# Seven products for eight: a third of an FFN's down projection by Strassen's scheme

## The chip, the core and the metric

The kernel runs on one core of a Trainium2 chip. The metric is the device time of one execution in microseconds; the time given is the median of several executions. The core has five engines with a queue each: TensorE (PE), VectorE (DVE), ScalarE (ACT), GpSimd (POOL) and SyncE (SP). Each works through its own queue in order, and they meet at semaphores.

## What is computed

Two blocks in a row on x, 256 tokens by 1024 columns, float32. The first is a Conformer-like block, and its FFN occurs twice:

```
def swiglu_ffn(x, w_gate, w_up, w_down):
    return (jax.nn.silu(x @ w_gate) * (x @ w_up)) @ w_down

x = x + 0.5 * swiglu_ffn(rmsnorm(x, ffn1_norm), ffn1_w_gate, ffn1_w_up, ffn1_w_down)
x = x + hybrid_mixer(rmsnorm(x, mix_norm), w_in, ...)
x = x + 0.5 * swiglu_ffn(rmsnorm(x, ffn2_norm), ffn2_w_gate, ffn2_w_up, ffn2_w_down)
x = rmsnorm(x, final_norm)
```

The second block is two attention mixers with layer norms ("fox", then "dsa"). The change concerns `@ w_down` in both FFNs: h, 256 x 2816, times a matrix of 2816 x 1024.

## The kernel before

**Precision.** Each float32 operand is cut in two parts, a rounded one (`hi`, type fp32r) and the rest (`lo`). A product is three matmuls: hi by hi, lo by hi, hi by lo.

**Weights.** The weights of the whole kernel are a list of units in the order of use, `unit_list`. A down unit is two k-tiles (of 128 rows each) by 512 columns: 128 x 1024 in the core's memory, 512 KB. `load` (line 205) puts it into one of four `raw` buffers over SP's queue (`N_RAW`). `prefetch` (line 187) casts it on ACT (`whi`, line 198) and subtracts on DVE (`wlo`, line 199), into one of eight pairs of buffers (`N_W`), at most eight units ahead of use (`AHEAD`). A raw buffer is free again when its `wlo` is written, a `whi`/`wlo` pair when PE has used it. `half` (line 216) multiplies one token tile (128 of the 256 tokens, t = 0 or 1) by one unit: six matmuls of 128x512, by way of `mm` (line 164, profile line L165).

**An FFN** (`ffn`, line 378) goes through gate and up in five chunks of 512 hidden columns and one of 256. Each chunk of h is written by DVE in 32x32 blocks transposed (`hb`, line 420). `regroup` sends it from POOL's queue through memory: four transfers `d<-hb` (line 285) and, once they have landed, one `hd<-d` (line 286). Later `put_h` cuts hd into `hh` on ACT and `hl` on DVE (`split_psum`, lines 240 and 241). These are h transposed, the stationary operands of down. `pin` keeps an instruction in the order of the program; `later` queues work for a time at which enough matmuls have been issued by the planner's count (`DUE`). The other instructions are put in order by a scheduler.

**Down** comes next. There are two halves n of 512 columns; in each, 11 units by two token tiles, 132 matmuls; 264 in an FFN. After the last unit of a half, x is added to (line 440). After the first half, `x_T(t, 0)` is queued: PE transposes half of x, DVE scales it (`xg`, line 247), ACT casts it (`xh`, line 248), DVE subtracts (`xl`, line 249). That is input of the next stage, the mixer ("mix") or the second block's first layer.

Of the kernel before, what the change touches and what calls it, by code (L numbers as in the profile page):

```python
# [9 lines left out]
F32 = mybir.dt.float32  # L10
# [23 lines left out]
AHEAD = 8  # L34

# [8 lines left out]
          (0, 512), (512, 512), (1768, 512), (2280, 512)]  # L44


def unit_list():

    u = []

    def block(m, c0, w, k0=0, k1=KT, n=None):
        n = n or (UK * (512 // w) if 512 % w == 0 else UK)
        for k in range(k0, k1, n):
            u.append((m, k, min(n, k1 - k), c0, w))

    def ffn(i):
        for c0, w in FFN_CH:
            block(f"gate{i}", c0, w, n=1 if i == 1 and c0 == 0 else None)
            block(f"up{i}", c0, w)
        for n in range(2):  # L60
            block(f"down{i}", 512 * n, 512, 0, FT)
# [26 lines left out]
    "ffn_x": 3.0,  # L88
    "mix_T": 9.32,
# [26 lines left out]
class Kern:  # L116
    def __init__(self, ctx, tc, A):
# [11 lines left out]
        self.raw, self.W = {}, {}  # L129
# [57 lines left out]
    def prefetch(self, splits):  # L187
        nc = self.nc
        for _ in range(splits):
            if self.n_split < min(len(UNITS), self.used + AHEAD):  # L190
                self.load(self.n_split)
                i = self.n_split
                raw = self.raw.pop(i)
                nk, w = UNITS[i][2], UNITS[i][4]
                hi = self.wp.tile([P, UK * 512], F32R, name="whi", tag="whi", bufs=N_W)
                lo = self.wp.tile([P, UK * 512], F32R, name="wlo", tag="wlo", bufs=N_W)
                m = nk * w
                nc.scalar.copy(hi[:, :m], raw[:, :m])  # L198
                nc.vector.tensor_sub(lo[:, :m], raw[:, :m], hi[:, :m].bitcast(F32))  # L199
# [5 lines left out]
    def load(self, upto):  # L205
        while self.n_dma <= min(upto, len(UNITS) - 1):
            i = self.n_dma
            m = UNITS[i][2] * UNITS[i][4]
            raw = self.wp.tile([P, UK * 512], F32, name="raw", tag="raw", bufs=N_RAW)
            w = self.A["w"]  # L210
            self.nc.sync.dma_start(out=raw[:, :m], in_=bass.AP(
                tensor=w.tensor, offset=w.offset + self.off[i], ap=[[m, P], [1, m]]))
            self.raw[i] = raw
            self.n_dma += 1

# [16 lines left out]
    def done(self, n):  # L232
        self.used = n

# [143 lines left out]
    def ffn(self, u, gain, next_gain):  # L378
        nc, tc = self.nc, self.tc
        with tc.tile_pool(name="ffn", bufs=1, reuse_waits="tile") as pool:  # L380
# [3 lines left out]

            def put_h(j, n, hd):
                for t in range(2):
# [40 lines left out]
            nd = FT // UK  # L427
            for n in range(2):
                accs = [self.bank("mm") for _ in range(2)]
                for i in range(nd):  # L430
                    if n == 0 and i == nd - 2:
                        self.drain()
                    for t in range(2):
                        self.half(accs[t], hT[t], u + i, i == 0, i == nd - 1)
                    self.done(u + i + 1)
                    self.prefetch(1)
                u += nd
                for t in range(2):
                    xs = self.x[t][:, 512 * n:512 * n + 512]
                    nc.vector.tensor_add(xs, xs, accs[t])  # L440
                    if n == 0:
                        self.later(DUE["ffn_x"], lambda t=t: self.x_T(t, 0, next_gain))
# [752 lines left out]
def layout(inp):  # L1195
# [15 lines left out]
    for m, k0, nk, c0, w in UNITS:  # L1211
        b = mats[m][k0 * P:(k0 + nk) * P, c0:c0 + w]
# [33 lines left out]
```

## Time and profile before

| | |
|---|---|
| median of 3 runs | 720.14 us (718.51 to 721.09) |
| the profiled execution | 717.48 us |
| its span in the trace | 715.7 us |
| mean granted clock of PE | 0.996 |
| PE busy | 98% of the span |
| DVE busy | 69% |
| ACT busy | 52% |
| POOL busy | 9% |

The span reaches from the first to the last instruction in the trace; 1.78 us of the profiled execution lie outside it. Down runs from 129.40 to 190.15 us in the first FFN and from 397.72 to 458.49 us in the second. In a row of the trace an instruction's duration reaches from its start to its end; those of one engine overlap a little, so the step from one to the next is shorter than the duration. A bracket says how long the engine had stood idle before the row and what ended it.

### The profile page before, as it was taken

How to read it: one execution, taken by the hardware profiler on the slowest of the kernel's cores; microseconds unless marked ns; L12 is line 12 of the kernel's file. 1: busy time of each engine (PE TensorE's matmuls, PEld its weight loads, DVE VectorE, ACT ScalarE, POOL GpSimd, SP SyncE). 2: the span in 40 equal slices, each digit the busy share in tenths (PEclk: the TensorE clock that was granted, in tenths of full speed). 3: DMA queues.
4: the chain of work that ended last, by engine and by line, in shares of the span. 5: the costliest groups of instructions: out<-in, count | busy, mean ns of one | idle time of the engine just before them, and what ended most of it. 6: DMA issues, size and time to landing. Idle time of an engine off the chain costs nothing.

```text
span 715.7 us, 9843 instructions
## 1 busy us (share of the span) xinstructions
PE 701.6 (98%) x3594; PEld 590.0 (82%) x3594; DVE 491.4 (69%) x790; ACT 368.8 (52%) x552; POOL 62.2 (9%) x90
## 2 busy tenths in 40 slices
PE   8999999999999999999999999999999999999995
PEld 6788888888888778888888888888898888778984
DVE  5867765576547878655865576555456968997965
ACT  6664544364546646353544364555465635675820
POOL 0101110200002001011110200000300001000001
PEclk9999999999999999999999999999999999999998
DMA  8888566876744435558656867555672527543501
GB/s 257 311 313 301 209 217 212 302 229 221 254 151 145 178 115 172 194 197 290 208 209 220 293 229 228 175 192 174 206 253 77 159 83 230 195 123 114 177 1 59
DMA packets 42305, 140.87 MB, mean 197 GB/s; under 512 B 5512, under 2 KB 6672, under 8 KB 42128
## 3 DMA queue, kind: packets, MB, share of 16 engines
q1 hardware_dynamic: 37728, 127.23, 52.9%
q0 software_dynamic: 4096, 12.60, 5.0%
q8 instruction: 28, 0.46, 0.3%
q10 hardware_dynamic: 432, 0.41, 0.2%
q14 instruction: 21, 0.17, 0.1%
HBM read 133.39 MB, written 6.82 MB: 196 GB/s over the span
## 4 chain that ended last, share of the span: by engine, by line
PE 89%; DVE 4%; DMA 4%; ACT 2%; issue 1%; POOL 0%; SPq 0%; DVEq 0%; ACTq 0%; POOLq 0%
PE mm L165 80%; PE sc L165 5%; PE tr L180 3%; DMA raw<-in_w 1%; DVE wlo L199 1%; DMA rope<-in_rope 1%; PE tr L165 1%; DMA xin<-in_xT 1%; ACT whi L198 1%; DMA gain<-in_gain 0%; ACT s L452 0%; DVE sel L994 0%; DVE sel L1003 0%; ACT xh L323 0%; DVE s L543 0%
## 5 line engine op out<-in xcount | busy, mean ns | idle before, releaser
L199 DVE TENSOR_TENSOR wlo<-raw,whi 128x1024 fp32r<-128x1024 f32 (+3 forms) x236 | 274.3, 1177 | 83.0 <-ACT whi L198 73.4
L198 ACT CAST whi<-raw 128x1024 fp32r<-128x1024 f32 (+3 forms) x236 | 235.2, 1013 | 126.9 <-PE mm L165 65.7
L165 PE MATMUL mm<-whi,xh 128*128 128x512 f32 (+3 forms) x760 | 288.4, 380 | 1.9 <-ACT whi L198 1.9
L165 PE MATMUL mm<-wlo,xh 128*128 128x512 f32 (+3 forms) x760 | 283.4, 373 | 0.1
L165 PE MATMUL mm<-whi,xl 128*128 128x512 f32 (+3 forms) x760 | 283.4, 373 | 0.0
L165 PEld LDWEIGHTS mm<-whi,xh 128*128 128x128 f32 x760 | 143.2, 188 | 25.7 <-ACT whi L198 3.7
L165 PEld LDWEIGHTS mm<-wlo,xh 128*128 128x128 f32 x760 | 143.1, 188 | 25.5 <-DVE wlo L199 1.9
L165 PEld LDWEIGHTS mm<-whi,xl 128*128 128x128 f32 x760 | 143.3, 189 | 22.4 <-DVE xl L249 0.2
L165 PE MATMUL mm<-whi,hh 128*128 128x512 f32 x176 | 68.7, 390 | 0.0
L165 PE MATMUL mm<-whi,hl 128*128 128x512 f32 x176 | 68.5, 389 | 0.0
L165 PE MATMUL mm<-wlo,hh 128*128 128x512 f32 x176 | 68.5, 389 | 0.0
L241 DVE TENSOR_TENSOR hl<-hd,hh 128x512 fp32r<-128x512 f32 (+1 forms) x24 | 14.5, 644 | 59.4 <-ACT hh L240 59.4
L240 ACT CAST hh<-hd 128x512 fp32r<-128x512 f32 (+1 forms) x24 | 12.9, 583 | 67.0 <-DMA hd<-d 67.0
L285 POOL DMA_DIRECT2D d<-hb x48 | 26.5, 558 | 149.2 <-DVE hb L420 149.1
L165 PEld LDWEIGHTS mm<-wlo,hh 128*128 128x128 f32 x176 | 33.0, 188 | 6.9
L165 PEld LDWEIGHTS mm<-whi,hh 128*128 128x128 f32 x176 | 33.1, 188 | 6.8
L165 PEld LDWEIGHTS mm<-whi,hl 128*128 128x128 f32 x176 | 33.1, 188 | 6.7
L407 ACT ACTIVATE th<-mm,hr 128x512 f32<-128x512 f32 (+1 forms) x24 | 15.5, 648 | 19.9 <-PE mm L165 18.8
L452 ACT ACTIVATE s<-s,nmax 128x128 f32<-128x128 f32 (+1 forms) x48 | 21.3, 446 | 7.0 <-DVE nmax L450 7.0
L299 POOL TENSOR_TENSOR rs<-ms,mhalf 128x1 f32<-128x1 f32 x10 | 6.5, 652 | 169.7 <-DVE ms L312 169.7
L299 POOL TENSOR_TENSOR lr<-ve,mhalf 128x1 f32<-128x1 f32 x4 | 4.0, 991 | 167.6 <-DVE ve L651 167.6
L409 DVE SCALAR_TENSOR_TENSOR a<-th,mm 128x512 f32<-128x512 f32 (+1 forms) x24 | 15.1, 628 | 5.0 <-ACT th L407 5.0
(219 smaller groups left out, 598.6 us busy)
## 6 DMA issues: line engine op xcount, KB each, us to landing
raw<-in_w SPq DMA_DIRECT2D x208, 512.0 KB, 4.6
d<-hb POOLq DMA_DIRECT2D x40, 128.0 KB, 4.7
hd<-d POOLq DMA_DIRECT2D x10, 512.0 KB, 6.5
raw<-in_w SPq DMA_DIRECT2D x12, 344.0 KB, 3.4
raw<-in_w SPq DMA_DIRECT2D x8, 372.0 KB, 3.5
raw<-in_w SPq DMA_DIRECT2D x8, 256.0 KB, 4.4
x<-in_x SPq DMA_DIRECT2D x2, 512.0 KB, 6.6
B<-in_bias SPq DMA_DIRECT2D x1, 1024.0 KB, 5.5
```

Of the source, the lines that this page charges most:

```text
L165: self.nc.tensor.matmul(out, a, b, start=start, stop=stop)
L180: self.nc.tensor.transpose(out, a, self.ident[:p, :p])
L198: nc.scalar.copy(hi[:, :m], raw[:, :m])
L199: nc.vector.tensor_sub(lo[:, :m], raw[:, :m], hi[:, :m].bitcast(F32))
L240: i = nc.scalar.copy(hi, src)
L241: j = nc.vector.tensor_sub(lo, src, hi.bitcast(F32))
L285: self.nc.gpsimd.dma_start(out=d[a].rearrange("b i m -> i b m"), in_=src[32 * a:32 * a + 32])
L299: self.nc.gpsimd.tensor_tensor(out, a, self.mhalf[:, 0:1].to_broadcast(list(a.shape)), op=ALU.pow)
L407: nc.scalar.activation(th[:, :w], acc[:, :w], AF.Tanh, scale=hr[t])
L409: nc.vector.scalar_tensor_tensor(a[t][:, :w], th[:, :w], 1.0, acc[:, :w], op0=ALU.add, op1=ALU.mult)
L452: nc.scalar.activation(s[:, h, :], s[:, h, :], AF.Exp, bias=m[:, h:h + 1], accum_out=l[:, col + h:col + h + 1])
```

## The change

The first eight of the 22 k-tiles of h and of w_down are seen as two by two blocks: A11, A12, A21, A22 (128 tokens by 512 hidden columns) and B11 to B22 (512 rows by 512 columns). Seven products of sums of such blocks stand for the eight plain ones:

| product | of h | of the weights | goes to |
|---|---|---|---|
| P1 | A11 | B11 | x(0,0), m |
| P5 | A21 − A22 | B11 + B12 | x(0,1), x(1,1) |
| P6 | a sum of blocks | P5's + B22 | m, then x(0,1) |
| P7 | A11 − A21 | B12 + B22 | m, then x(1,0), x(1,1) |
| P2 | A12 | B21 | x(0,0) |
| P4 | A22 | P6's + B21 | x(1,0) |
| P3 | a sum of blocks | B22 | x(0,1) |

Signs are taken up in the sums; x(t, n) is token tile t, column half n. Each product is 12 matmuls, in two halves g of two k-tiles (`prod`), so 84 for 96. The 14 other k-tiles stay direct, as 14 units. The list `DOWN` sets the order: six direct units, then products and direct units by turns, then two direct units.

- Eight weight blocks of 512 KB are loaded in place of the eight units, not into raw buffers but to stay: b11 and b12 in the buffers of the old x transposed, b22 in those of hb, b21 in those of hd. b11, b12 and b22 are loaded when down opens.
- Their sums are made on DVE in place (line 230), eight of 128x1024 in each FFN. Each product half is split like a unit, 14 instead of 8.
- The four sums of h and their splits are made during gate and up, from the time at which the second chunk's h is cut, 2 us apart by the planner's count (`DUE["ffn_sum"]`); one split of h that nobody needs falls away.
- Additions to x (line 542): 13 of 128x512 instead of 4 in each FFN; one copy into m (ACT) and two additions to m (DVE).
- `x_T(t, 0)` is queued behind P4.

The core of the diff:

```
+AHEAD_P = 5
+DOWN = [(0, 8), (1, 8), (0, 10), (1, 10), (0, 12), (1, 12), "P1", (0, 14), "P5", (1, 14), "P6", (0, 16), "P7",
+        (0, 18), "P2", (0, 20), "P4", (1, 16), "P3", (1, 18), (1, 20)]
...
             if self.n_split < min(len(UNITS), self.used + AHEAD):
-                self.load(self.n_split)
                 i = self.n_split
-                raw = self.raw.pop(i)
+                if i in RECIPE and (not self.open_down or RECIPE[i][0] == "P1" and i >= self.used + AHEAD_P):
+                    break
+                self.load(i)
                 nk, w = UNITS[i][2], UNITS[i][4]
+                if i in RECIPE:
+                    what, g = RECIPE[i]
+                    w = 512
+                    _, add, key = PROD[what]
+                    raw = self.block[key, g]
+                    if add:
+                        self.pin(nc.vector.tensor_add(raw, raw, self.block[add[1], g]))
+                else:
+                    raw = self.raw.pop(i)
...
+                a = nc.scalar.copy(hi[:, :m], raw[:, :m])
+                b = nc.vector.tensor_sub(lo[:, :m], raw[:, :m], hi[:, :m].bitcast(F32))
+                if i in RECIPE:
+                    self.pin(a), self.pin(b)
...
+    def prod(self, acc, lhs, i):
+        if i not in self.W:
+            self.prefetch(i + 1 - self.n_split)
+        hi, lo = self.W[i]
+        g = RECIPE[i][1]
+        xh, xl = lhs
+        for k in range(2):
+            kk = 2 * g + k
+            self.mm(acc, xh[:, kk, :], hi[:, k, :], kk == 0, False, 1)
+            self.mm(acc, xl[:, kk, :], hi[:, k, :], False, False, 1)
+            self.mm(acc, xh[:, kk, :], lo[:, k, :], False, kk == 3, 1)
+        self.pump()
...
+            self.fpool, self.block, self.open_down = pool, {}, True
+            for i in range(u, len(UNITS)):
+                if i in RECIPE and RECIPE[i][0] in ("P1", "P5", "P6") and UNITS[i][0] == UNITS[u][0]:
+                    self.load_block(i)
...
+            for what in DOWN:
+                if what in PROD:
+                    acc = self.bank("sc")
+                    for g in range(2):
+                        self.prod(acc, lhs[what], u)
+                        u += 1
+                        self.done(u)
+                        self.prefetch(2)
+                    if what == "P1":
+                        nc.scalar.copy(m, acc)
+                    elif what in ("P6", "P7"):
+                        nc.vector.tensor_add(m, m, acc)
+                    for t, n, op in goes[what]:
+                        to_x(t, n, m if what in ("P6", "P7") else acc, op)
+                    if what == "P4":
+                        for t in range(2):
+                            self.later(DUE["ffn_x"], lambda t=t: self.x_T(t, 0, next_gain))
+                    continue
```

What stands in a row on three engines and places. First ACT's queue around the last h casts of the first FFN (`hh0` and `hh1` are the casts for the two token tiles, of the chunk of 512 and then of the one of 256 columns). Before:

```order
L198 CAST whi_1383<-raw_1333 128x1024
L240 CAST hh0_80<-hd_1100 128x512
L240 CAST hh1_82<-hd_1100 128x512
L198 CAST whi_1401<-raw_1351 128x1024
L198 CAST whi_1419<-raw_1369 128x1024
L240 CAST hh0_80<-hd_1250 128x256
L240 CAST hh1_82<-hd_1250 128x256
L198 CAST whi_1437<-raw_1387 128x1024
```

And in the changed kernel, at the same place:

```order
L315 CAST hh0_80<-hd_1114 128x512
L315 CAST hh1_82<-hd_1114 128x512
L315 CAST hh0_80<-hd_1264 128x256
L315 CAST hh1_82<-hd_1264 128x256
L236 CAST whi_1348<-b110_1271 128x1024
L236 CAST whi_1352<-b111_1273 128x1024
L236 CAST whi_1368<-raw_1330 128x1024
L236 CAST whi_1373<-b110_1271 128x1024
```

The two weight casts between the chunks' h casts are gone, and the casts of P1's halves (from b110 and b111) come behind the last h cast. Next DVE's queue behind the last h split (`hl`); b120 and b121 are the two halves of B12. Before:

```order
L241 TENSOR_TENSOR hl0_81<-hd_1250,hh0_80 128x256
L241 TENSOR_TENSOR hl1_83<-hd_1250,hh1_82 128x256
L199 TENSOR_TENSOR wlo_1438<-raw_1387,whi_1437 128x1024
L199 TENSOR_TENSOR wlo_1456<-raw_1405,whi_1455 128x1024
L199 TENSOR_TENSOR wlo_1478<-raw_1423,whi_1477 128x1024
L199 TENSOR_TENSOR wlo_1518<-raw_1441,whi_1517 128x1024
```

And in the changed kernel:

```order
L316 TENSOR_TENSOR hl0_81<-hd_1264,hh0_80 128x256
L316 TENSOR_TENSOR hl1_83<-hd_1264,hh1_82 128x256
L237 TENSOR_TENSOR wlo_1349<-b110_1271,whi_1348 128x1024
L237 TENSOR_TENSOR wlo_1353<-b111_1273,whi_1352 128x1024
L237 TENSOR_TENSOR wlo_1369<-raw_1330,whi_1368 128x1024
L230 TENSOR_TENSOR b110_1271<-b110_1271,b120_1275 128x1024
L237 TENSOR_TENSOR wlo_1374<-b110_1271,whi_1373 128x1024
L230 TENSOR_TENSOR b111_1273<-b111_1273,b121_1277 128x1024
L237 TENSOR_TENSOR wlo_1393<-b111_1273,whi_1392 128x1024
L237 TENSOR_TENSOR wlo_1397<-raw_1377,whi_1396 128x1024
```

Between the subtractions stand the sums of blocks, each ahead of the cast and the subtraction that use it. Last ACT's queue around the casts of x's first half (`xh` from `xg`). In the kernel before they stand in the middle of down, behind the cast of a down unit of the second column half:

```order
L198 CAST whi_1589<-raw_1539 128x1024
L198 CAST whi_1607<-raw_1557 128x1024
L248 CAST xh0_1489<-xg_1496 128x512
L248 CAST xh1_1500<-xg_1507 128x512
L198 CAST whi_1625<-raw_1575 128x1024
```

In the changed kernel they stand at down's end, among the casts of the mixer's weights:

```order
L236 CAST whi_1685<-raw_1643 128x1024
L236 CAST whi_1720<-raw_1658 128x1024
L236 CAST whi_1732<-raw_1670 128x1024
L323 CAST xh0_1698<-xg_1705 128x512
L323 CAST xh1_1709<-xg_1716 128x512
L236 CAST whi_1751<-raw_1689 128x1024
```

The casts of x moved from the middle of down to behind the weight casts of the next stage, the first of which PE uses right behind down.

## Rows read from the trace of the kernel before

**Rows 1.** The page, busy time, share of the span and instructions of each engine.
```profile
PE 701.6 (98%) x3594; PEld 590.0 (82%) x3594; DVE 491.4 (69%) x790; ACT 368.8 (52%) x552; POOL 62.2 (9%) x90
```

**Rows 2.** What PE waited for: us in total, times, longest.
```profile
PE mm L165 <- ACT whi L198: 1.9, 3, 1.2
...
PE sc L165 <- DVE s L543: 0.2, 1, 0.2
```

**Rows 3.** Windows over both down stages: busy us (instructions) by engine, clock, DMA share.
```profile
core 0: us, PE busy (x) PEld busy (x) DVE busy (x) ACT busy (x) POOL busy (x), PEclk, DMA share, GB/s
129.40:190.15 60.75, 60.75 (x274) 50.34 (x273) 36.54 (x40) 26.81 (x30) 3.68 (x6) 1.00 0.71 238
397.72:458.49 60.77, 60.77 (x274) 50.40 (x273) 36.03 (x40) 26.29 (x30) 3.68 (x6) 1.00 0.70 231
```

**Rows 4.** Timeline of PE at down's end: start, duration, line, operation.
```profile
182.67 0.39 PE L165 MATMUL mm<-whi,hh 128*128 128x512 f32 x1
...
190.15 0.39 PE L165 MATMUL mm<-whi,xh 128*128 128x512 f32 x1
```

**Rows 5.** Groups by line and form: busy us, mean ns of one | idle before.
```profile
L199 DVE TENSOR_TENSOR wlo<-raw,whi 128x1024 fp32r<-128x1024 f32 x208 | 250.3, 1219 | 72.3 <-ACT whi L198 62.8 <-PE mm L165 7.4
...
L198 ACT CAST whi<-raw 128x1024 fp32r<-128x1024 f32 x208 | 214.5, 1050 | 109.2 <-PE mm L165 51.4 <-DMA raw<-in_w 45.7 <-issue 8.0
```

**Rows 6.** Timeline of DVE in down of the first FFN.
```profile
143.02 1.29 DVE L241 TENSOR_TENSOR hl<-hd,hh 128x512 fp32r<-128x512 f32 x2 [6.93 <-ACT hh L240]
144.49 2.36 DVE L199 TENSOR_TENSOR wlo<-raw,whi 128x1024 fp32r<-128x1024 f32 x2 [0.18 <-ACT whi L198]
...
160.31 1.28 DVE L440 TENSOR_TENSOR x<-x,mm 128x512 f32<-128x512 f32 x2
161.51 1.22 DVE L199 TENSOR_TENSOR wlo<-raw,whi 128x1024 fp32r<-128x1024 f32 x1
```

**Rows 7.** Timeline of DVE in gate and up, one chunk.
```profile
66.72 0.68 DVE L409 SCALAR_TENSOR_TENSOR a<-th,mm 128x512 f32<-128x512 f32 x1
74.04 1.29 DVE L241 TENSOR_TENSOR hl<-hd,hh 128x512 fp32r<-128x512 f32 x2 [6.64 <-ACT hh L240]
```

**Rows 8.** Timeline of ACT around the last h casts, first and second FFN.
```profile
147.53 0.71 ACT L240 CAST hh<-hd 128x256 fp32r<-128x256 f32 x2 [2.12 <-DMA hd<-d]
148.15 3.07 ACT L198 CAST whi<-raw 128x1024 fp32r<-128x1024 f32 x3
...
416.61 0.71 ACT L240 CAST hh<-hd 128x256 fp32r<-128x256 f32 x2 [2.55 <-DMA hd<-d]
417.23 4.05 ACT L198 CAST whi<-raw 128x1024 fp32r<-128x1024 f32 x4
```

**Rows 9.** Timeline of POOL: an earlier chunk, and the last of the first FFN.
```profile
60.55 2.19 POOL L285 DMA_DIRECT2D d<-hb  x4 [17.97 <-DVE hb L420]
67.33 0.76 POOL L286 DMA_DIRECT2D hd<-d  x1 [4.59 <-DMA d<-hb]
...
135.35 2.18 POOL L285 DMA_DIRECT2D d<-hb  x4
144.40 0.76 POOL L286 DMA_DIRECT2D hd<-d  x1 [6.87 <-DMA d<-hb]
```

**Rows 10.** The page's transfers: KB each, median us from issue to landing.
```profile
raw<-in_w SPq DMA_DIRECT2D x208, 512.0 KB, 4.6
...
hd<-d POOLq DMA_DIRECT2D x10, 512.0 KB, 6.5
```

**Rows 11.** Timelines of PE and ACT where x's first half is made in down.
```profile
163.42 1.03 PE L180 MATMUL tr<-cst,x 128*128 128x128 f32 x8
...
164.97 1.22 ACT L248 CAST xh<-xg 128x512 fp32r<-128x512 f32 x2 [1.89 <-DVE xg L247]
```

**Rows 12.** Windows behind PE's last matmul: columns as in rows 3.
```profile
707.00:708.00 1.00, 0.21 (x2) 0.00 (x1) 0.72 (x2) 0.00 (x0) 0.00 (x0) 1.00 0.00 0
...
710.00:711.00 1.00, 0.00 (x0) 0.00 (x0) 1.00 (x3) 0.00 (x0) 0.00 (x0) 0.71 0.03 8
711.00:712.00 1.00, 0.00 (x0) 0.00 (x0) 0.49 (x2) 0.00 (x0) 0.00 (x0) 0.50 0.44 168
```

More of the change, by code (lines that the diff above doesn't have):

```diff
@@ L59, in ffn @@
             block(f"up{i}", c0, w)
-        for n in range(2):
-            block(f"down{i}", 512 * n, 512, 0, FT)
+        for what in DOWN:
+            if what in PROD:
+                for g in range(2):
+                    k, c = PROD[what][0] or (0, None)
+                    RECIPE[len(u)] = (what, g)
+                    u.append((f"down{i}", k + 2 * g, 2, 512 * (c or 0), 0 if c is None else 512))
+            else:
+                n, k = what
+                u.append((f"down{i}", k, 2, 512 * n, 512))
     ffn(1)
@@ L207, in load, with load_block, load_to @@
             i = self.n_dma
+            if i in RECIPE and not self.open_down:
+                return
             m = UNITS[i][2] * UNITS[i][4]
[L209 to L213, printed above, removed]
-            self.n_dma += 1
+            self.n_dma += 1
+            if i in RECIPE:
+                what, g = RECIPE[i]
+                if m and (LOADS[what], g) not in self.block:
+                    self.load_block(i)
+                continue
+            raw = self.raw[i] = self.wp.tile([P, UK * 512], F32, name="raw", tag="raw", bufs=N_RAW)
+            self.load_to(raw, i, m)
+    def load_block(self, i):
+        what, g = RECIPE[i]
+        raw = self.block[LOADS[what], g] = self.new_block(LOADS[what], g)
+        self.load_to(raw, i, UK * 512)
+    def load_to(self, raw, i, m):
+        w = self.A["w"]
+        self.nc.sync.dma_start(out=raw[:, :m], in_=bass.AP(
+            tensor=w.tensor, offset=w.offset + self.off[i], ap=[[m, P], [1, m]]))
     def half(self, acc, lhs, i, first, last, kbase=0, cols=None):
@@ new lines, in ffn, with to_x @@
+            accs = {}
+            def to_x(t, n, acc, op=ALU.add):
+                xs = self.x[t][:, 512 * n:512 * n + 512]
+                nc.vector.tensor_tensor(xs, xs, acc, op=op)
+            for what in DOWN:
+                if what in PROD:
+                    acc = self.bank("sc")
+                    for g in range(2):
+                        self.prod(acc, lhs[what], u)
[11 more added lines that the diff above has]
+                            self.later(DUE["ffn_x"], lambda t=t: self.x_T(t, 0, next_gain))
+                    continue
+                n, k = what
+                if k == FT - 2 and n == 0:
+                    self.drain()
+                for t in range(2):
+                    if k == 8:
+                        accs[t, n] = self.bank("mm")
+                    self.half(accs[t, n], hT[t], u, k == 8, k == FT - 2)
+                u += 1
+                self.done(u)
+                self.prefetch(2)
+                if k == FT - 2:
+                    for t in range(2):
+                        to_x(t, n, accs[t, n])
```

70 lines of the change are left out of this document (51 added, 19 removed).

## The prediction

> **What bounds the kernel now.** First I read the busy line: TensorE (PE) is busy for 701.6 of 715.7 us, VectorE (DVE) 69%, ScalarE (ACT) 52% [rows 1]. Then the list of PE's waits: its largest entry is 1.9 us, its last 0.3 [rows 2]. The two windows, one for each stage of down products, show PE busy for the whole stretch, 60.75 and 60.77 us, at a granted clock of 1.00, while DVE is busy for 36 us and the DMA engines for 70% [rows 3]. So here the time is a count of matmuls times a pace, and DVE has 24 us to spare over the whole stage. Whether it has them at the right places is another matter, and that decides this change. The pace: 33 matmuls from 182.67 to 190.15 us make 0.2267 us for one of 128x512 [rows 4]. At 190.15 the next stage's first matmul starts without a gap.
>
> What one split unit (128x1024) costs stands in the groups by form: 1.05 us for the cast on ACT, 1.22 for the subtraction on DVE [rows 5]. In a row they overlap: a pair of subtractions takes 2.36, so a further one costs 2.36 − 1.22 = 1.14 [rows 6]. A pair of 128x512 additions to x is followed by the next row 1.20 later, so 0.60; I take 0.61 [rows 6].
>
> **1. What is saved.** Seven products of 12 matmuls stand for 96: 84, so 12 fewer in each FFN. Twice 12 × 0.2267 = **−5.44 us**, 2.72 in each, all on PE's path [rows 3, 4].
>
> **2. What costs nothing.** Weight bytes are equal: eight blocks for eight units. The four sums of h and their splits (some 5 us of DVE, less one split of h) go into the gate and up stage. There DVE stands idle for 6.64 us before the h splits of a chunk, and the wait ends with ACT's cast, not with PE [rows 7]; one such hole lies in each chunk of 512, and the sums are queued from there on, 2 us apart by the planner's count. If that cover were gone, they would cost up to 5 us in each FFN. The cast of P1 into m (one on ACT) hides in ACT's idle half.
>
> **3. Wait at P1.** In the order, the splits of P1's two halves stand behind the splits of the last h chunk on ACT and DVE, and only the six direct units are split ahead of it. On ACT the last h casts wait for the transfer hd<-d, and end late: they begin at 147.53, and the next whi begins at 148.15 [rows 8]. Ahead of it the casts were idle for 2.12 us, and DVE, in the same place, for 6.93 [rows 6, 8]. Before, this cost PE nothing, since the weights of eight units were split. Now PE has 72 matmuls for six units: 129.40 + 72 × 0.2267 = 145.7 [rows 3, 4], and P1's first weights are there at 148.15 + 1.05 = 149.2 [rows 5, 8]. PE waits **3.5 us**. In FFN2 P1's first half is split ahead of the last h chunk, so PE gets six matmuls further, to 397.72 + 78 × 0.2267 = 415.4, and the second half's weights come at 417.23 + 1.05 = 418.3: **2.9 us** [rows 3, 8]. Queued behind the same casts on ACT and DVE are all splits that follow, the direct units' too.
>
> The unknown is when hd lands, with the blocks' loads beside it. Early end: POOL's d<-hb pieces of this chunk start at 135.35 and hd<-d at 144.40; in an earlier chunk it was 60.55 to 67.33, 6.8 instead of 9.05 [rows 9]. That takes 2.3 off: 1.2 us. Late end: the landing here took 147.53 − 144.40 = 3.1 us for 256 KB, the median of the 512 KB ones is 6.5 [rows 10], which adds 3.4: 6.9 us. I stay at 3.5 and 2.9, as the rows stand in the same place.
>
> **4. DVE's chain from P1 to P7.** This is the largest term. From P1's first subtraction to P7's first, DVE has in its order 10 subtractions, 6 sums of blocks and 5 rows of 128x512 (four additions to x and one to m). No row of before shows a sum of two f32 blocks; the nearest is the subtraction of the same shape, from f32 to fp32r, so 1.14 each. That is 16 × 1.14 + 5 × 0.61 = 21.3. P5 asks for two round trips: sum on DVE, cast on ACT, subtraction on DVE, with nothing between, 1.05 for the cast [rows 5] and some 0.15 around it: 2.4. With the tail of the last subtraction (0.08) that is 23.8 us. PE's work over the same piece (P1, two direct units between, P5, P6, a third direct unit, and the two matmuls of P7 that want no wlo) is 74 × 0.2267 = 16.8. So PE loses **7.0 us** more. In FFN2 the chain starts one subtraction and six matmuls later: 22.6 − 15.4 = **7.2**. Bounds: one less for sums at 0.98 and one more for sums at 1.30, so 6 to 8. DVE's idle time of before does not help, since it lies ahead of the last h split (6.93 us) and in the stage's second half.
>
> In the rows, adjacent subtractions overlap: the second of a pair costs 1.14 [rows 6]. [...]
>
> **5. The next stage's first input.** The transposes of x's first half stood after the first column half and hid under the second. Now this half is only whole near the end (the last product that adds to it is P4), and its transposes stand in P3 and the last direct unit. On ACT the casts of xh stand behind two whi casts whose loads need raw buffers that DVE frees late. Counted from the start of P7's first subtraction: 14 subtractions, 2 sums and 6 small rows stand ahead of the subtraction that frees the second of these buffers: 16 × 1.14 + 6 × 0.61 = 21.9. Then itself 1.22, a landing of 4.6 [rows 10], a cast of 1.05 and the xh cast of 0.61 [rows 5, 11] (half of the pair at 164.97): 29.4. PE has 1.22 + 106 × 0.2267 + 0.8 for eight transposes [rows 11] = 26.05. PE waits **3.4 us** at the first matmul of the next stage. Lower end: if DVE is not late, only the chain behind the last transposes counts; before, it ran from the transposes' end at 164.45 to the casts' end at 166.19 = 1.74, and with three to four matmuls still queued (0.9) 0.8 is left [rows 11]. Upper end: a landing of 6.5 instead of 4.6 [rows 10]: 5.3.
>
> **Sum.** FFN1: −2.7 + 3.5 + 7.0 + 3.4 = +11.2. FFN2: −2.7 + 2.9 + 7.2 + 3.4 = +10.8. Together +22.0 on the profiled execution's 717.48: 739.5. The median of the runs, 720.14, lies 2.66 above that execution, so **742.0**. All low ends: 2 × (−2.7 + 1.2 + 6.0 + 0.8) = +10.6, 730.7. All high ends: 2 × (−2.7 + 6.9 + 8.0 + 5.3) = +35.0, 755.1.
>
> **The rivals.**
> *Faster: the saved matmuls show.* If DVE's chain began 7 us before PE reaches P1, at 138.7, PE would never wait, and the time would be 720.14 − 5.44 = **714.7**. The place is the last h split: it would have to be done by then. For it: DVE and ACT stand idle ahead of it and the blocks are loaded early. Against it: the transfer landed at 147.5 and 416.6 [rows 8], 9 us too late, and the splits behind it are tied in order. It comes out faster than before only where the waits of a stage together stay under 2.7 us. 10%, some of it within 0.3%.
> *The clock falls.* Behind the last matmul (707.2 us) PE's granted clock stays 1.00 for some 3 us, and is 0.71 in the slice from 710 and 0.50 after [rows 12]. Waits of 3.5 and 3.4 us are about as long. [...] Against: DVE's chain breaks most of the wait into pieces of about 1 us. 11%. [...]
> *The sums stall gate and up.* 2 × 5 more, **752**; against it the holes [rows 7]. 3%.
>
> **How the numbers follow.** My forecast has 76%. The range 730 to 755 holds it with all its bounds and the two slower rivals; outside lies the faster one. A measurement of this kernel can tell about 0.3% (2.2 us) from no change. Faster by more than that: 0.07; within: 0.03; slower: 0.90.
>
> **What would show it.** Right: 24 fewer matmuls; in each down stage waits of PE on ACT's whi at P1 (3.5) and on whi and wlo at P5, P6 and P7 (together 7), and one on xh at the next stage; DVE busy without a hole from P1 on. In all, each down stage about 70 to 72 us long. Wrong: hd landing by 140; a sum on DVE far from 1.14; a clock under 1.00 in a window of down; PE's waits in gate and up grown; or a down stage under 61 us.

## The result and the profile after

The changed kernel takes **750.11 us** (median of 4 runs, 747.75 to 752.02), the kernel before 719.33 (718.43 to 721.09) beside it: ratio 1.0423 [1.0386, 1.0461], slower. The profiled execution took 747.75 us with a span of 746.0, against 717.48 and 715.7. The span grew by 30.3 us.

The page's busy line, with the columns of [rows 1]:

```profile
PE 709.6 (95%) x3570; PEld 588.4 (79%) x3570; DVE 543.7 (73%) x854; ACT 383.6 (51%) x572; POOL 64.9 (9%) x90
```

The 24 matmuls are gone (x3594 to x3570), and PE is still busy 8 us longer: some of the matmuls ran slower, and behind a pause a matmul counts with its whole length (0.4 to 0.8 us) and not with its step of 0.2267. DVE has 64 instructions and 52 us more. What PE waited for (us in total, times, longest), which was 1.9 us at its largest entry before [rows 2]:

```profile
PE sc L193 <- ACT whi L236: 10.7, 6, 6.0
PE mm L193 <- ACT xh L323: 5.2, 3, 2.6
PE sc L193 <- DVE wlo L237: 3.8, 7, 0.8
PE mm L193 <- ACT whi L236: 2.2, 5, 0.7
PE mm L193 <- DVE a L509: 1.2, 1, 1.2
```

`sc` is a bank of a product's sum, so the first and third entries are P1 to P7; the second is the next stage's first input. The two down stages as windows, each from its first matmul to the next stage's first one, the columns of [rows 3]:

```profile
130.94:206.68 75.74, 62.60 (x263) 48.16 (x261) 53.99 (x61) 32.20 (x37) 4.90 (x9) 0.95 0.50 176
416.01:486.24 70.23, 62.29 (x263) 48.34 (x261) 51.64 (x56) 30.87 (x35) 3.69 (x6) 0.98 0.51 177
```

Before, these were 60.78 and 60.77 us with PE busy throughout and DVE for 36 [rows 3] (down's first matmul starts at 129.37, 0.03 ahead of the window there). Now PE stands idle for 13 and 8 us, and DVE has 54 and 52 us of work.

**The account.** The span grew by 1.57 us ahead of the first down stage, 14.96 in it (75.74 − 60.78), 1.76 from there to the second, 9.46 in that (70.23 − 60.77), and 2.55 behind it: 30.3. The first stage in PE's timeline, at its turning points (start, duration, line, operation, in brackets the idle time before and what ended it):

```profile
130.94 0.40 PE L193 MATMUL mm<-whi,hh 128*128 128x512 f32 x1
...
133.69 0.50 PE L193 MATMUL mm<-whi,hh 128*128 128x512 f32 x1 [1.21 <-DVE a L509]
...
154.96 0.80 PE L193 MATMUL sc<-whi,hh 128*128 128x512 f32 x1 [6.00 <-ACT whi L236]
...
179.00 0.50 PE L193 MATMUL sc<-wlo,s 128*128 128x512 f32 x1 [0.59 <-DVE wlo L237]
...
206.68 1.32 PE L193 MATMUL mm<-whi,xh 128*128 128x512 f32 x2 [2.35 <-ACT xh L323]
```

The rows are down's first matmul, a pause at the second unit, P1's first matmul, P7's third, and the next stage's first. Without waits P1 would begin 72 × 0.2267 = 16.32 us after down's start, at 147.26; it begins 7.70 later. From P1 to P7's third matmul it is 24.04, for 16.8 of PE's work: 7.2 lost. From there to the next stage it is 27.68, for 24.83 of work (26.05, less the 1.22 that the prediction counts to P7's first subtraction): 2.9 lost. −2.72 + 7.70 + 7.2 + 2.9 = 15.1, and 14.96 was measured. The same points of the second FFN:

```profile
435.46 0.50 PE L193 MATMUL sc<-whi,hh 128*128 128x512 f32 x1 [1.59 <-ACT whi L236]
...
458.37 0.50 PE L193 MATMUL sc<-wlo,s 128*128 128x512 f32 x1 [0.54 <-DVE wlo L237]
...
486.24 1.31 PE L193 MATMUL mm<-whi,xh 128*128 128x512 f32 x2 [2.58 <-ACT xh L323]
```

P1 is 435.46 − (416.01 + 78 × 0.2267) = 1.77 late, the chain takes 22.91 for 15.4 (7.5 lost), and the last piece 27.87 for 24.83 (3.0): −2.72 + 1.77 + 7.5 + 3.0 = 9.6; measured 9.46.

**P1's wait** begins on POOL and ACT. POOL's issue of the last hd, and ACT behind it:

```profile
138.55 2.18 POOL L360 DMA_DIRECT2D d<-hb  x4
147.70 0.76 POOL L361 DMA_DIRECT2D hd<-d  x1 [6.96 <-ACT hh L315]
```

```profile
153.24 0.71 ACT L315 CAST hh<-hd 128x256 fp32r<-128x256 f32 x2 [6.11 <-DMA hd<-d]
153.86 1.99 ACT L236 CAST whi<-b 128x1024 fp32r<-128x1024 f32 x2
```

hd lands 5.5 us after its issue (3.1 before [rows 8, 9]), and the issue stands 16.8 us behind down's start instead of 15.0. From d<-hb to hd<-d it is 9.15 us, about as before (9.05 [rows 9]), so the bracket's name, ACT, is not what made the issue late: d<-hb itself starts 7.6 us behind down's start instead of 6.0. P1's weights have to wait for the h casts.

At the next stage's first input ACT's queue reads, at down's end:

```profile
203.48 1.05 ACT L236 CAST whi<-raw 128x1024 fp32r<-128x1024 f32 x1 [1.41 <-DMA raw<-in_w]
205.06 1.05 ACT L236 CAST whi<-raw 128x1024 fp32r<-128x1024 f32 x1 [0.52 <-DMA raw<-in_w]
206.01 1.14 ACT L323 CAST xh<-xg 128x512 fp32r<-128x512 f32 x2
```

DVE had written xg by 204.8, but the casts of xh stand behind two weight casts that wait for their loads.

**DVE's chain** from P1 on, at its first two round trips:

```profile
158.35 1.22 DVE L230 TENSOR_TENSOR b<-b,b 128x1024 f32<-128x1024 f32 x1
160.76 1.23 DVE L237 TENSOR_TENSOR wlo<-b,whi 128x1024 fp32r<-128x1024 f32 x1 [1.20 <-ACT whi L236]
161.91 1.22 DVE L230 TENSOR_TENSOR b<-b,b 128x1024 f32<-128x1024 f32 x1
164.32 1.23 DVE L237 TENSOR_TENSOR wlo<-b,whi 128x1024 fp32r<-128x1024 f32 x1 [1.19 <-ACT whi L236]
165.47 1.22 DVE L237 TENSOR_TENSOR wlo<-raw,whi 128x1024 fp32r<-128x1024 f32 x1
166.60 1.22 DVE L230 TENSOR_TENSOR b<-b,b 128x1024 f32<-128x1024 f32 x1
```

A sum of two blocks lasts 1.22 us and steps on after 1.14 (166.60 to the next row at 167.74), as the subtractions do. The two brackets are P5's round trips: sum on DVE, cast on ACT, subtraction on DVE.

**The clock** fell behind P1's wait in the first FFN and behind both waits on xh:

```profile
155.00:160.00 5.00, 4.96 (x14) 3.51 (x15) 4.57 (x4) 2.12 (x3) 0.00 (x0) 0.65 0.42 132
206.68:212.00 5.32, 5.32 (x17) 4.22 (x18) 5.32 (x7) 2.56 (x3) 0.40 (x1) 0.71 1.01 395
486.24:492.00 5.76, 5.76 (x18) 4.51 (x19) 5.76 (x7) 2.42 (x3) 0.00 (x0) 0.70 0.79 285
```

The matmuls there stand 0.43 us apart instead of 0.2267 until 158.5, 209.85 and 489.80; over these pieces the granted clock is 0.50, 0.52 and 0.52, and behind the last two it is 1.00 again. The last two pieces hold 7 and 8 matmuls in 3.17 and 3.56 us: 3.17 − 7 × 0.2267 = 1.6 and 3.56 − 8 × 0.2267 = 1.7 lost, straight on the path, and they make most of the 1.76 and 2.55 us outside the stages. Behind P1's wait the slow clock costs little, because DVE's chain is later than PE there anyway.

In the second FFN it did not fall behind P1's wait (1.59 us; the clock is 1.00 from 435.46 to 440) but later, inside the chain, where no wait is longer than 1.1 us:

```profile
443.70 0.50 PE L193 MATMUL sc<-whi,hh 128*128 128x512 f32 x1 [1.10 <-ACT whi L236]
...
444.96 0.55 PE L193 MATMUL sc<-wlo,hh 128*128 128x512 f32 x1 [0.53 <-DVE wlo L237]
445.31 0.63 PE L193 MATMUL sc<-whi,hh 128*128 128x512 f32 x1
...
448.71 0.39 PE L193 MATMUL mm<-wlo,hh 128*128 128x512 f32 x1
```

From 445.31 to 448.71 eight matmuls stand 0.43 us apart, at a clock of 0.50. So short pieces of waiting, one behind the other, did not keep the clock up here.

### The profile page after: what moved, and what is told of

It is laid out like the page before. It is cut to its first block, busy times and chain, and to the rows that moved or that the text cites. A ratio compares the mean times of both kernels' runs of the same rounds, so it can differ in the third digit from the quotient of the medians.

```text
span 746.0 us, 9904 instructions
## 1 busy us (share of the span) xinstructions
PE 709.6 (95%) x3570; PEld 588.4 (79%) x3570; DVE 543.7 (73%) x854; ACT 383.6 (51%) x572; POOL 64.9 (9%) x90
## 4 chain that ended last, share of the span: by engine, by line
PE 50%; DVE 20%; DMA 16%; issue 6%; ACT 4%; POOL 3%; DVEq 0%; SPq 0%; ACTq 0%; POOLq 0%
PE mm L193 42%; DVE wlo L237 9%; DMA raw<-in_w 6%; DMA d<-hb 5%; PE sc L193 5%; DMA hd<-d 4%; PE tr L208 3%; DVE b L230 2%; ACT whi L236 2%; POOL d L360 2%; DVE x L542 1%; PE tr L193 1%; DMA xin<-in_xT 1%; POOL hrs L374 1%; DVE h L518 1%
## 5 line engine op out<-in xcount | busy, mean ns | idle before, releaser
L237 DVE TENSOR_TENSOR wlo<-raw,whi 128x1024 fp32r<-128x1024 f32 (+3 forms) x220 | 256.0, 1179 | 56.0 <-ACT whi L236 43.0
L236 ACT CAST whi<-raw 128x1024 fp32r<-128x1024 f32 (+3 forms) x220 | 219.2, 1012 | 111.0 <-DMA raw<-in_w 61.7
L236 ACT CAST whi<-b 128x1024 fp32r<-128x1024 f32 x28 | 28.8, 1052 | 41.9 <-DVE b L230 33.2
L193 PE MATMUL mm<-whi,hh 128*128 128x512 f32 x112 | 44.6, 398 | 1.6 <-DVE a L509 1.2
L193 PE MATMUL mm<-whi,hl 128*128 128x512 f32 x112 | 44.1, 394 | 0.0
L193 PE MATMUL mm<-wlo,hh 128*128 128x512 f32 x112 | 43.4, 392 | 0.0
L237 DVE TENSOR_TENSOR wlo<-b,whi 128x1024 fp32r<-128x1024 f32 x28 | 33.6, 1220 | 11.8 <-ACT whi L236 11.8
L193 PEld LDWEIGHTS mm<-whi,hh 128*128 128x128 f32 x112 | 21.3, 190 | 7.2 <-DVE a L509 1.6
L193 PEld LDWEIGHTS mm<-whi,hl 128*128 128x128 f32 x112 | 21.3, 190 | 4.4
L193 PE MATMUL sc<-whi,hh 128*128 128x512 f32 x32 | 13.9, 434 | 9.1 <-ACT whi L236 9.1
```

Source lines behind the costliest of these rows:

```text
L193: self.nc.tensor.matmul(out, a, b, start=start, stop=stop)
L236: a = nc.scalar.copy(hi[:, :m], raw[:, :m])
L237: b = nc.vector.tensor_sub(lo[:, :m], raw[:, :m], hi[:, :m].bitcast(F32))
```

## The experiments

Each number is the median of its runs; the kernel before gave 718.4 to 719.1 beside them. "Stage" is the length of a down stage, 60.78 and 60.77 before and 75.74 and 70.23 after.

**e1: P1 ahead of the last h split.** The splits of the last two h chunks are queued later, so that P1's weights are cast and subtracted first.

```
-self.later(DUE["ffn_T"], ... put_h(j, n, hd))
+self.later({4: 22.0, 5: 17.0}.get(j, DUE["ffn_T"]), ... put_h(j, n, hd))
```

> The changed kernel, with one thing different: the splits of the last two h chunks are queued 10 to 15 us later, so that the splits of P1 and P5 and the first sums of weight blocks stand ahead of them on ACT and DVE. My theory (P1's splits wait behind the last h split, and DVE's chain from P1 to P7 starts too late because of it): the chain starts some 7 us after down opens instead of 24, PE is no longer waiting at P1 (6.2 and 1.7 us in the changed kernel) nor between P1 and P7 (7.2 and 7.5), so 720 us, between 716 and 726. Rival (the chain is simply too much work for DVE wherever it starts, or the loads of the blocks set it): P1's wait goes, the 7 us stay, 735 to 742. Rival (the lower clock sets the loss): above 740.

Measured 732.42 (ratio 1.0192 [1.0171, 1.0213]), stages 66.28 and 64.63. P1's wait is gone and the chain begins 12.7 us earlier, at 142.28. 17.7 of the 30.8 us come back, not all: the time lies between the expected range and the rival's, in neither. What PE waited for:

```profile
PE sc L193 <- DVE m L555: 4.4, 2, 2.2
PE sc L193 <- DVE x L542: 2.3, 4, 1.2
```

```profile
131.37:197.65 66.28, 61.57 (x263) 48.54 (x262) 54.90 (x62) 32.99 (x38) 4.90 (x9) 0.97 0.58 209
```

A new wait stands in the place of the old one, which the expectation had missed: P2's first matmul needs the bank of an earlier product, and DVE's addition into m, which empties it, is queued behind the splits. From 142.28 on, DVE's queue has no gaps but three round trips of 1.2 us until 184. That what is left goes with DVE's load and not with its start, e8 below shows: without the sums it is gone.

**e2: the after kernel without the sums of weight blocks.** One line changes.

```
-                    if add:
+                    if add and False:
```

> The changed kernel without the eight sums of weight blocks in each FFN: each product uses its first block alone, so what it computes is no longer the down product. My theory (DVE's chain of 10 subtractions, 6 sums and 5 small rows with two round trips is what PE waits for behind P1): without the sums the chain is 14.5 us against 16.8 us of matmuls, so the 7.2 and 7.5 us go, and some 2 us at the next stage's first matmul; P1's own wait (6.2 and 1.7 us) stays. 726 us, between 722 and 732. Rival (PE waits for the casts, the loads or x's additions, not for the sums): above 740.

Measured 731.16 (1.016 [1.0117, 1.0204]), stages 66.68 and 66.74. The chain's waits and those on xh are gone; the wait at P1 stays, about 6 us in both FFNs:

```profile
PE sc L193 <- ACT whi L236: 12.5, 2, 6.6
```

So the sums cause terms 4 and 5, and term 3 is a cause of its own. The second FFN's wait is 5.88 us where 1.7 had been expected: here P1's first half, too, is split behind the last h. Behind both waits the matmuls run 0.43 us apart (mean granted clock of the run 0.988, 0.996 in the kernel before), and without the chain to cover it this shows too.

**e8: both together** (e1's edit and e2's).

> The late-split kernel without the sums of weight blocks (so what it computes is no longer the down product): what the scheme would give if its sums of weights were free and its splits came in time. My theory (the waits of the late-split kernel come from DVE's work, 9.1 us of sums in each FFN and two round trips through ACT): no wait of a microsecond or more in down but the one for the banks of gate and up at its second unit (1.2 us), so 718 us: 719 less 5.4 of matmuls, with 1.2 to 2 us in each FFN for that wait and the transposes at the end. Rival (even so the products' additions and copies hold the banks): 724 or more.

Measured 715.94 (718 was expected), 0.9963 [0.9946, 0.998], stages:

```profile
132.59:191.66 59.07, 58.34 (x263) 48.07 (x261) 49.14 (x58) 33.62 (x38) 4.88 (x9) 1.00 0.69 244
399.24:457.30 58.06, 58.06 (x263) 48.15 (x261) 47.57 (x53) 33.53 (x36) 3.68 (x6) 1.00 0.64 227
```

The second stage is 60.77 − 58.06 = 2.71 us shorter: the saving of term 1, to the digit. This is the ceiling in this order: with seven products for eight and no price for the sums of weights, the kernel gains 2.6 us. It is not 5.4, since the first stage has a pause of 0.9 us and down opens 3.2 us later in the profiled execution. The two causes nearly add up: e1's edit gives back 17.7 us, e2's 19.0, both 34.2.

**e3: the kernel before, with x's first half transposed at the end of down.**

```
-                    if n == 0:
-                        self.later(DUE["ffn_x"], lambda t=t: self.x_T(t, 0, next_gain))
+                    if n == 1 and i == nd - 2:
+                        for t in range(2):
+                            self.later(DUE["ffn_x"], lambda t=t: self.x_T(t, 0, next_gain))
```

> The kernel before, with the transposes of x's first half moved to the end of down, as in the changed kernel; nothing else. My theory (the wait there in the changed kernel, 2.9 and 3.0 us, comes from DVE being late with the subtraction that frees a raw buffer, on top of a short chain of its own): here DVE is not late, and only the chain of transposes, xg, xh, xl is open, 0.8 us in each FFN, so 721 us, at most 723. Rival (the place of the transposes costs the whole wait, and the clock falls behind it): 3 us and 1.7 us of lower clock in each FFN, 728 to 730.

Measured 719.81 (1.0014 [0.9998, 1.003]). In the trace the late transposes cost 0.46 us in one FFN and 0.44 in the other (the pair of the next stage's first two matmuls takes 1.08 us and 1.06, a pair elsewhere 0.62); the measured time is not clear of no change. So most of the 2.35 and 2.58 us in the changed kernel comes from DVE being late, and in e2, where DVE is not, that wait is gone.

**e4: the after kernel with ten matmuls of no use between down and the next stage**, so that PE is busy while it waits for xh.

```
+            idle = self.bank("sc")
+            for k in range(10):
+                self.mm(idle, hT[1][0][:, 20, :], hT[1][0][:, 16:20, :], k == 0, k == 9, 1)
```

> The changed kernel with ten matmuls of 128x512 on old operands, whose result nobody reads, between the last matmul of down and the first of the next stage, 2.3 us of work in each FFN where PE waits 2.4 and 2.6 us for xh. My theory (PE's idle time there is what makes the granted clock fall behind it, at a cost of 1.7 us in each FFN): the clock stays at 1.00 there, and the time is 3 to 4 us shorter, 746 us. Rival (the clock falls for another reason, such as the earlier waits or what the next stage does): no gain, the same time to 2 us more.

Measured 747.13 (1.0399 [1.0353, 1.0445]): the interval holds both the expected gain and none. The trace, of the slowest of the four runs, decides on the mechanism. Windows from the next stage's first matmul, in both FFNs:

```profile
209.66:215.00 5.34, 5.31 (x22) 4.23 (x23) 4.14 (x5) 2.38 (x3) 0.00 (x0) 1.00 0.93 359
491.38:497.00 5.62, 5.60 (x23) 4.44 (x24) 5.62 (x7) 3.32 (x4) 0.00 (x0) 1.00 0.85 278
```

The clock is 1.00 where it was 0.71 and 0.70, and 22 matmuls fit where there were 17. So it is PE's idling that lets the clock fall there. What it is worth in total these runs don't settle.

**e5: e1, with the sums on POOL.**

```
-                        self.pin(nc.vector.tensor_add(raw, raw, self.block[add[1], g]))
+                        self.pin(nc.gpsimd.tensor_tensor(raw, raw, self.block[add[1], g], op=ALU.add))
```

> The late-split kernel (last h splits queued later, 732.4 us), with the sixteen sums of weight blocks on POOL instead of DVE. In that kernel DVE has no hole from 142.3 us to the end of down. Theory A (what is short is DVE's own time): 8 x 1.14 = 9.1 us less for DVE in each FFN, the waits behind DVE (1.8 us at P7, 2.4 at P2, with the clock's fall behind it) go, 722 us. Theory B (the sums cost DVE as much from another engine): DVE's subtractions beside a sum on POOL take longer than 1.22 us, and the time is that of the late-split kernel or more, 731 to 745. I hold B for likelier. [...]

Measured 748.25 (1.0411 [1.0384, 1.0439]): as slow as the changed kernel, and above the ranges of both theories. The groups of the sums and of the subtractions beside them (busy us, mean ns of one):

```profile
L230 POOL TENSOR_TENSOR b<-b,b 128x1024 f32<-128x1024 f32 x16 | 46.9, 2952 | 16.0 <-DMA b<-in_w 10.7 <-DVE wlo L237 5.3
L237 DVE TENSOR_TENSOR wlo<-b,whi 128x1024 fp32r<-128x1024 f32 x28 | 45.8, 1638 | 27.1 <-ACT whi L236 27.0
```

And PE's largest entry:

```profile
PE sc L193 <- DVE x L542: 16.1, 2, 10.1
```

POOL takes 2.95 us for a sum, and while it works DVE's own work is held up. Two rows of DVE, one just ahead of a series of four sums on POOL (158.24 to 171.4), one beside it:

```profile
158.08 1.21 DVE L237 TENSOR_TENSOR wlo<-raw,whi 128x1024 fp32r<-128x1024 f32 x1
159.22 6.71 DVE L237 TENSOR_TENSOR wlo<-b,whi 128x1024 fp32r<-128x1024 f32 x2
```

A subtraction goes from 1.2 to about 3.3 us there. DVE is not relieved: the 16 sums are gone (19.3 us in the changed kernel), and yet it is busy for 550.5 us, 8.3 more than in e1 (542.2), since its splits take longer: those of blocks 1.64 us in the mean against 1.22 in the changed kernel, those of h at 128x512 1.01 against 0.69. The additions that free a product's bank come late behind them, and PE waits 10.1 us for one in the first FFN and 6.1 in the second. Why DVE's rows lengthen beside a sum on POOL, no run isolates.

**e6: e1, with P2, P4 and P3 summed in the banks of the direct units**, so that PE, not DVE, adds them; P4 moves ahead of a direct unit, and x's transposes are queued behind that unit.

```
+                    into = {"P2": (0, 0), "P4": (1, 0), "P3": (0, 1)}.get(what)
+                    acc = accs[into] if into else self.bank("sc")
```

> The late-split kernel, with P2, P4 and P3 accumulated into the PSUM banks of the direct units that go to the same part of x, in place of banks and additions of their own: three additions to x fewer on DVE in each FFN (1.8 us), and none of the three takes one of the two banks that PE waited for (2.2 us at P2 in both FFNs, 1.2 at P3 in the second, behind additions that stand late in DVE's queue). P4 goes ahead of the last direct unit of the first column half for that. My theory (with the chain started early, the banks held by late additions are the next wait, and the clock falls behind it): P2's and P3's waits and 1.4 us of lower clock in each FFN go, 724 us, 720 to 727. Rival (DVE's total work sets the stage, so a wait that is taken away comes back at the next splits): 729 to 732.

Measured 731.6 (1.019 [1.0165, 1.0215]). P2's bank wait is gone and the time is that of e1, as the rival had it (729 to 732): waits came up at P4's splits (1.29 and 0.53 us in the first FFN, 1.07 and 0.57 in the second) and at x's transposes (1.13; 1.60, 1.15). One wait removed, the next in the line takes its place.

**e9: e6, with each sum one unit earlier in DVE's queue**, so that its round trip is covered. `next_sum` makes the sum for the next product half whose block is free, right behind the unit's own subtraction.

```
-                    if add:
-                        self.pin(nc.vector.tensor_add(raw, raw, self.block[add[1], g]))
+                    self.block_sum(i)
...
                 self.n_split += 1
+                self.next_sum(i)
```

> The kernel with PSUM accumulation (731.6 us), with each sum of weight blocks put one unit earlier in DVE's queue, so that another unit's subtraction stands between a sum and the subtraction that needs its cast. My theory (DVE has no time to spare in down, and the three round trips sum, cast, subtraction leave it idle for 1.2 us each, 3.6 us in each FFN): these holes close, PE's waits behind DVE in down (4 to 5 us in each FFN) go down by about as much, 725 us, 722 to 728. Rival (the sums now wait for blocks that have not landed, or the waits are set by something other than DVE's load): 730 or more.

Measured 725.78 (1.0125 [1.0069, 1.018]; one of the four runs took 732.06, and the interval overlaps e6's a little), as expected; stages 62.14 and 65.68. The round trips are gone, and so are all large waits but one, on P6's bank:

```profile
PE sc L193 <- DVE x L561: 7.9, 2, 5.7
```

The bank is emptied by an addition to x (L561 in this kernel) that is queued on DVE behind splits and sums: 2.19 us in the first FFN and 5.70 in the second.

**e10: e9, with eight direct units ahead of P1 instead of six**, P1 and P5 one behind the other, and the h splits queued 3.5 to 5 us later.

```
+DOWN = [(0, 8), (0, 10), (0, 12), (1, 8), (1, 10), (1, 12), (0, 14), (1, 14), "P1", "P5", (0, 16), "P6", (0, 18), "P7",
+        (1, 16), "P2", "P4", (0, 20), "P3", (1, 18), (1, 20)]
```

> The kernel with the sums one unit earlier, and another order: eight direct units ahead of P1 in place of six, the first three of one column half and then three of the other (so that the fourth, not the second, needs the PSUM banks that gate and up still hold), P1 and P5 one behind the other; the h splits 4 us later. My theory (DVE stands idle for 6.3 us after down opens until B11 lands, and PE waits 1.1 us for the banks at the second unit): two more direct units are split in that hole, PE comes to P1 5.4 us later, the wait for banks goes, 718 us, 715 to 722, near the 716 of the kernel without sums. Rival (DVE is short of time over the whole stage, and a later P1 only moves the waits to its end): 724 to 729.

Measured 725.62 (1.0095 [1.0065, 1.0125]): no gain over e9; the rival's range (724 to 729) holds it, the expected one does not. Its stages:

```profile
130.45:191.64 61.19, 58.65 (x263) 47.81 (x261) 53.80 (x59) 31.72 (x36) 4.45 (x8) 1.00 0.64 229
401.70:465.12 63.42, 60.26 (x262) 49.23 (x261) 54.21 (x59) 32.79 (x37) 4.68 (x8) 0.97 0.63 225
```

DVE is busy for 54 of 61 us in the first. The bank wait stands at 2.48 and 2.45 us.

**e12: e10, with P1 and P5 copied from their banks by ACT**, so that the banks are free at once.

```
-                    if what == "P1":
-                        nc.scalar.copy(m, acc)
+                    if what in ("P1", "P5"):
+                        o = m if what == "P1" else m5
+                        nc.scalar.copy(o, acc)
+                        acc = o
```

> The kernel of the other order (725.6 us), with P1's and P5's results copied from PSUM by ACT, and added to x from that copy. In it PE waits once in each FFN, 2.6 us, for the bank that P6 takes: the addition of P1 to x stands late in DVE's queue; in the second FFN the clock falls behind it for 1 us. My theory (what is left is banks held by additions that DVE comes to late, and not DVE's whole load): both waits go, 719 us, 717 to 721: the same as the kernel before within what can be measured, and 2 to 4 us above the one without sums. Rival (DVE's whole load): the wait moves to P7, P2 or the next stage, 723 to 727.

Measured 725.67 (1.0085 [1.0053, 1.0117]): the bank wait is gone and nothing is gained. Waits of 0.51 and 1.54 us stand at x's transposes, 1.55 at xh, 1.01 at gate and up's bank. The time lies in the rival's range (723 to 727): that DVE's load, not any one wait, now sets the stage fits it, but is argued, since no run takes work off DVE in this kernel. The nearest is e1 against e8: without the 16 sums 16.5 us come back. DVE itself also waits here for blocks to land (2.47 us at one sum of the first FFN), and that share of the loads was not separated.

**e7 and e11: is hd late because the blocks are loaded beside it?** e7 loads only P1's block when down opens; e11 does the same and exchanges two blocks' buffers.

```
-                if i in RECIPE and RECIPE[i][0] in ("P1", "P5", "P6") and ...
+                if i in RECIPE and RECIPE[i][0] in ("P1",) and ...
```

> The changed kernel, with only B11 loaded when down opens; B12 and B22 are loaded in their turn. Theory (the part of P1's wait that I had put too low, 6.2 us in the first FFN instead of 3.5, comes from the block loads: they keep the DMA engines busy while hd<-d moves, which took 5.5 us to land instead of 3.1): hd lands 2 to 3 us earlier, P1's wait in the first FFN is 3 to 4 us, and if B12 and B22 are still there in time, the whole is 3 to 5 us shorter, 746 us. Rival (the landing of hd has nothing to do with the blocks, or the loads are now late for the sums): P1's wait stays at 6, or a new wait of DVE on the blocks eats the gain: 750 us or more.

> The changed kernel with B12 and B21 in exchanged buffers: B12 now goes where hd was, so that its load, and all loads behind it on SP's queue, come only when the last h is split. It is there for one number, the landing of the last hd<-d: 5.5 us after its issue in the changed kernel, 3.1 in the kernel before; the run with later block loads had not moved them in time (1.05 MB moved beside hd in both). Theory (the block loads beside it take it 2.4 us longer): it lands 3 to 3.7 us after its issue and P1's wait is 3.5 to 4.5 us. Rival (the landing depends on something else): 5 us or more, and P1's wait stays at 6. The whole time is longer in both cases, since P5's sums then wait some 5 us for B12: 752 to 760.

Measured 750.98 (1.0463 [1.0432, 1.0494]) and 752.69 (1.0474 [1.0436, 1.0512]), with waits at P1 of 6.05 and 5.93 in the first FFN. Neither edit did what it was meant to: 1.05 MB of weights still moved beside hd (0.11 MB in the kernel before), and hd landed 4.9 and 5.2 us after its issue. So the edits decide nothing. But the traces of the other runs say something. Wherever the cast of the last hd waits for its landing, the time from issue to landing goes with the weights that move meanwhile: 3.1 to 3.2 us beside 0.11 to 0.25 MB (both FFNs of the kernel before, the first of e3), 4.8 to 5.5 beside 1.05 MB (the changed kernel, e2, e4, e7, e11 and the second FFN of e3), 5.9 and 6.7 beside 1.57 MB (e8). e3 has no block loads at all; its windows from issue to landing, with the columns of [rows 3]:

```profile
146.13:149.26 3.13, 3.13 (x16) 2.58 (x15) 2.04 (x2) 0.59 (x2) 0.76 (x1) 1.00 0.52 164
414.69:420.17 5.48, 5.48 (x26) 4.54 (x25) 0.25 (x1) 0.00 (x1) 0.76 (x1) 1.00 0.69 239
```

hd lands later where more weights move beside it (164 and 239 GB/s in all), be they blocks or ordinary units. No edit took that traffic away, so that it is the cause is likely and not shown by a change.

## Why the prediction was right, and where its sizes were off

The forecast was 742.0, slower with 90%, with a range of 730 to 755; 750.11 came. In the span it was +22.0, and +30.3 was measured. Three slips on the way change nothing: 720.14 + 22.0 is 742.1; the last entry of PE's waits is 0.2 and not 0.3 [rows 2]; and the 6.93 us of idle DVE stand ahead of the split of 128x512, the last but one, not of the last [rows 6], but no term uses them. By its steps:

1. **Saved** (−5.44): right. 24 matmuls fewer, and e8's second stage is 2.71 us shorter where 2.72 was reckoned.
2. **Costs nothing**: mostly right. The first down stage opens 1.57 us later. 0.6 of it was there in the kernel's first 25 us, ahead of anything the change touches; one pause of 0.8 at 127.96, where gate and up wait for DVE's `h`, makes most of the rest. Such a pause, 0.5 to 2.2 us in all, stands in eight of the twelve kernels with the scheme and in neither of the two without, e8 (no sums of weights) included, so "nothing" was a little too low. In the other kernels with the scheme the opening lay between 0.4 us earlier and 4.6 later than before, and what the sums of h have to do with it was not isolated. The rival in which the sums stall gate and up had 10 us for the two FFNs; that did not come.
3. **Wait at P1** (3.5 and 2.9): the mechanism is right, and e2 shows it alone. The size was off: P1 began 7.7 and 1.8 us late. The transfer's place was taken from before; in the first FFN hd was issued 1.8 us later against down's start and took 2.4 us longer to land, together the 4.2 us by which the wait was longer; in the second it was issued 3.0 us earlier (12.7 us behind down's start instead of 15.7) and took 1.8 longer. The high end (6.9) had only the landing in it, and 7.7 lies above it. That the second FFN came out near 2.9 is in part luck: the wait there was 3.17 in e4, 4.43 in e7 and 5.88 in e2. A pause of 1.2 us at the second unit, on a bank that gate and up still held (the new order opens four sums at once), was not in the sum either; it is hidden, since P1's weights come later still.
4. **DVE's chain** (7.0 and 7.2): right, 7.2 and 7.5. A sum steps by 1.14, as taken from the nearest row; a single row lasts 1.22. The 0.15 us that the prediction put around the cast was its author's estimate, without a row of before; in the changed kernel the two round trips leave DVE idle for 1.20 and 1.19, with 1.05 for the cast. e2, without the sums, has none of the chain's waits.
5. **The next stage's first input** (3.4 each): right, 2.9 and 3.0, with xh behind two weight casts as reckoned. e3's trace puts the late transposes alone at 0.5.
6. **The clock** was given 11% as a rival and no place in the sum. It came true in addition to the forecast, not in its place: that is the step that failed. The slow clock makes 3.3 us of the 8.3 that were missing. The waits on xh that term 5 itself predicted (2.35 and 2.58 us) are followed by 7 and 8 matmuls at 0.43 us, 1.6 and 1.7 us lost; e4 shows that the clock stays up (1.00) when PE is kept busy. Behind P1's wait it fell as well (0.50), under DVE's cover, and in the second FFN inside the chain: the argument against it, that the chain breaks the wait into pieces of about 1 us, did not hold.

So of the 8.3 us between forecast and span, P1 makes 4.2 − 1.1 = 3.1, the chain 0.5, xh −0.9, the late opening 1.6, and the two pieces outside the stages 1.76 + 2.55 = 4.3, of which the slow clock is 3.3; the remaining −0.3 is what the two stages' sums above miss of the lengths measured, and rounding.

One thing the prediction did not ask is what would be left if the waits were mended. e1, e6, e9, e10 and e12 answer it: from 750 to 725.6, with no single run under 720.7, where the kernel before has 718 to 719. DVE has 54 us of work in a stage in which PE has 58, tied to PE by banks, buffers and round trips. Each mended wait brought the next one up.

## What to carry to other kernels

A scheme that saves matmuls by adding sums pays on another engine: here 12 matmuls, 2.7 us of PE in an FFN, were bought with eight sums of 1.14 us, six more splits and eleven small additions on DVE, and an idle share of 40% on that engine was no cover, because the new work had to be done between two given matmuls. Early on, leave the sums out and run that, with the splits in good time: e8 gives the ceiling of this order (0.4%) in one run, while e2, with the late splits, does not. And when a forecast has PE waiting, as here for 2.2 to 2.6 us or for a row of shorter pieces, price the slower matmuls behind the wait together with the wait, with a chance of their own.

## What was unexpected of the hardware

- PE's clock fell behind waits of 2.2 to 2.6 us (0.43 us between matmuls, for 7 or 8 of them in the changed kernel), but not at every such wait: in e1 it fell behind 2.24 us in the first FFN and not behind 2.20 in the second, and in e10 behind 2.45 in the second FFN and not behind 2.48 in the first. In the changed kernel it also fell behind pieces of 1.10 us and less. The length of the wait alone does not decide it; what does, these runs don't show.
- A sum of 128x1024 f32 on POOL takes 2.95 us in the mean beside DVE's work, and DVE's subtraction of the same shape rises from 1.22 to 1.64 in the mean of the 28 from blocks, to 3.3 in a series. Where DVE hardly works beside POOL (DVE stands idle for 6.72 us until 151.30), two sums from 147.78 take 4.76 us in e5, 2.38 each: 2.38 / 1.218 = 1.95 times the mean of DVE's sums in the changed kernel. In the mean, with DVE at work, it was 2952 / 1218 = 2.4 times.
- Two h splits of 128x512 that take 1.3 us on DVE [rows 6] took 3.46 beside a sum on POOL.
